# A hybrid decoder layer on one core: second-half norm by single tiles, two projections by turns, and a new order of small instructions on ScalarE and VectorE

## The chip, the cores and the metric

The kernel runs on one core of one Trainium2 chip. The metric is device time in microseconds (us) of one execution. The core has a matmul engine (TensorE, "PE" in the profile, its weight loads "PEld"), VectorE ("DVE"), ScalarE ("ACT"), GpSimd ("POOL") and SyncE ("SP", which issues DMAs). Each runs its own instructions strictly in the order in which they stand, and waits at semaphores for the others. Matmul results land in PSUM banks; a bank can be written again once DVE or ACT has copied it out.

## The reference, cut to what matters

One layer over 512 prompt rows and 8 x 4 sample rows, 1024 wide:

```python
x = layer_norm(ALPHA * x + 0.5 * swiglu(x, ffn1...), ln1_g, ln1_b)
proj = x @ w_in
ps_mix = ps + mu_shift * (prev - ps)           # prev: the row before
r, k, v, wd, ad, gd = slices of ps_mix
decay = exp(-exp(-softplus(-(w0 + tanh(wd) @ w_lora_up)) - 0.5))
a = sigmoid(a0 + ad @ a_lora_up);  g = sigmoid(gd) @ g_lora_up
kk = k * k_k;  kk = kk / max(sqrt(sum(kk * kk)), 1e-12)
k = k * (1 + (a - 1) * k_a)
o, wkv_new = wkv7_recurrence(r, decay, k, v, kk, a, wkv0)
y_rwkv = (group_norm(o) + sum(r * k * r_k) * v) * g
z = cw[0]*u[t-2] + cw[1]*u[t-1] + cw[2]*u[t];  y_conv = c_b * z      # u = c_c * c_h
x = layer_norm(ALPHA * x + concat(y_rwkv, y_conv) @ w_out, ln2_g, ln2_b)
x = layer_norm(ALPHA * x + 0.5 * swiglu(x, ffn2...), ln3_g, ln3_b)
```

## The kernel before

**Layout.** Channels lie on the 128 partitions, rows along the free axis: 544 rows in two halves, 256 (first) and 288 (second). Every weight matmul is done in three parts with both operands split into a rounded high half and a remainder: for each 128-channel tile of the input, `mm3` (L150 to L152) issues high x high, high x low, low x high. One projection of one half is 24 such matmuls. The split of an input tile is one ACT copy (L138) and one DVE subtraction (L139); the split of a weight tile is the pair L134, L135.

**The first norm.** `layer_norm` is run half by half. For the second half, once the reciprocal deviation is there (`rs`, two ACT instructions L255 and L258, tile `cpb`), it goes over the eight channel tiles in four pairs: DVE multiplies a pair (L262), ACT scales one tile (L268) and DVE the other (L266), then the pair is split for the projections. While that goes on, first-half projections fill PE; the second-half projections follow: 12 (`T12`, the inputs of decay and `a`), 13 (`sgd`, of the gate), 4 (`k` of pair 0), 0 (`r`).

**Projections.** `project` has 24 matmuls, then ACT evicts the bank (L880, L882, L883, tiles `pb` and `dt`), and DVE mixes each row with the one before (L884, L888).

**Pairs.** The eight heads are four pairs. For a pair, `gates` (L947, L950) makes the decay's sigmoid `sw` and `a`; `square` (L956) squares the pair's `k`; `norms` (L962, L963) sums the squares on PE and clamps them on DVE; `decays` makes a running sum on DVE (L969, tile `Pn`) and its exponentials on ACT (L974 to L978), with a table load ahead (L123); `prep` (L990 to L1001) makes the operands of the recurrence on DVE: `AR` and `nk` (the normalized keys), `a` rescaled (L994), the key times `a` (L997) and the products in `bkb` (L998, L999). ACT's sigmoids of the next pair write the tile of `a` that L997 is the last to read.

**Scores and chains.** `scores` (L1018 to L1061) makes each pair's triangular products, transposes `bkb` and `v` into `BK` and `UV`, and copies them out on ACT (L1037, L1053). `elim` solves small triangles on DVE and sends them over DRAM to `DM` and `O` (DMAs of L1093), from which `rounds` (L1123) doubles the block size on PE. Then a chain over eight chunks carries the state; in each chunk PE multiplies (L1195), DVE and ACT copy the result to `UV` (L1196, L1197), and PE goes on (L1204).

**Conv.** `conv` does the short convolution, three projections for each 128 channels; `conv_taps` holds the three taps: the first on ACT (L1335), the other two on DVE (L1337), each for the prompt's 512 columns and the samples' 32.

**What sets the order.** Each engine's instructions stand in the order in which the code issues them. `weave` and `drain` take background generators from a queue (`bg`) and put portions of their matmuls between the steps of a critical one; `seq` runs generators one after the other, `alt` lets them take turns at each of their `yield`s. A `tc.issue_after(x)` lets the instructions within it go behind `x` and not ahead; otherwise a scheduler is free to place an instruction anywhere its data allow. A pair's preparation runs as background (`own_a`, `own_b`) behind the pair before.

Of the kernel before, what the change touches and what calls it, by code (L numbers as in the profile page):

```python
# [19 lines left out]
P = 128  # L20
# [41 lines left out]
def body(ctx: ExitStack, tc: tile.TileContext, xT, gu1, wd1, win, wo_c, wo_0, wo_1, gu2, wd2, wl, ln3, eye, lora, vec, cst,  # L62
# [58 lines left out]
    def issue(prev, f, *args, **kw):  # L121
        with tc.issue_after(prev.ins):
            return f(*args, **kw)  # L123
# [32 lines left out]
    bg = deque()  # L156
    seen = dict(pe=None, fill=None, new=[], old=[])

# [53 lines left out]

    def layer_norm(z, c0, c1, gcol, bcol, epsv, q, rs, s1, sink, table=None, hl2=None, both=False):
        n = c1 - c0
# [44 lines left out]
        yield 1200 if pair else 600  # L259
        for d in range(0, KD, 2):  # L260
            zz = z[:, d:d + 2, c0:c1]
            DVE.tensor_tensor(zz, zz, rs[:, None, :n].to_broadcast([P, 2, n]), op=OP.mult)  # L262
            for e in (d, d + 1):
                x, g, b = z[:, e, c0:c1], col(gcol, e), col(bcol, e)
                if both and e > d:
                    DVE.tensor_scalar(x, x, g, b, op0=OP.mult, op1=OP.add)  # L266
# [22 lines left out]
    def to_x(spill):  # L289
        def sink(d, x, c0, c1):  # L290
            split(xhl[:, 0, d:d + 2, c0:c1], xhl[:, 1, d:d + 2, c0:c1], x)
            if spill:
                dma(xsp[:, d:d + 2, c0:c1], x)
        return sink
# [533 lines left out]
    drain()  # L828
    ln1b = layer_norm(z, *HALF[1], V_LN1G, V_LN1B, epsf, lnq, f1.lnr, f1.s1[1], to_x(True), None, f1.hl2, True)
    ss = keep.tile([P, 14, NSEQ], F32, name="sst")  # L830
# [32 lines left out]
    def s4(x):  # L863
        return x.rearrange("p (b t) -> p b t", t=4)

    def project(i, mt, h, x):
        c0, c1 = HALF[h]
        w = wget(i)
        q = big()
        yield from mm3(q[:, :c1 - c0], w, xhl, range(KD), c0, c1)  # L870
        pb = pp.tile([P, 297], F32, name="pb", bufs=2)
        d = pp.tile([P, 288], F32, name="dt", bufs=2)
        t0 = 256 * h
        pv = pb[:, 257:297].rearrange("p (b t) -> p b t", t=5)
# [5 lines left out]
        ACT.activation(pb[:, 1:257], q[:, :256], AF.Copy)  # L880
# [3 lines left out]
        DVE.scalar_tensor_tensor(x[:, t0:t0 + 256], pb[:, 0:256], col(V_MU, mt), d[:, 0:256], op0=OP.mult, op1=OP.add)  # L884
        if h == 0:
            POOL.tensor_copy(car[:, mt:mt + 1], pb[:, 256:257])
        else:
            DVE.scalar_tensor_tensor(s4(x[:, 512:544]), pv[:, :, 0:4], col(V_MU, mt), s4(d[:, 256:288]),  # L888
                                     op0=OP.mult, op1=OP.add)
# [44 lines left out]
    class Pair:  # L934
# [18 lines left out]

        def square(self, kf):
            self.kq = kq = p2.tile([P, 576], F32, name="kq")
            ACT.activation(kq, kf, AF.Square, scale=col(V_KK, self.p))  # L956

# [7 lines left out]
        def decays(self):  # L965
            p, kq = self.p, self.kq
            self.Pi = Pi = p2.tile([P, 600], F32, name="Pi")
            self.Pn = Pn = p2.tile([P, 576], F32, name="Pn")
            DVE.tensor_tensor_scan(Pn, keepm, self.sw, 0.0, op0=OP.mult, op1=OP.add)  # L969
# [4 lines left out]
            ln_exp(self.sg, lambda: ACT.activation(pi[:, :, 1:65], s64(Pn[:, :512]), AF.Exp, scale=-CDEC))  # L974
            ACT.activation(ps_[:, :, 1:5], s4(Pn[:, 512:]), AF.Exp, scale=-CDEC)
# [7 lines left out]
        def prep(self, kf, rf, vf):  # L983
# [12 lines left out]
            DVE.tensor_tensor(s4(AR[:, pl, 8, 1, :]), s4(rf[:, 512:]), ps_[:, :, 1:5], op=OP.mult)  # L996
            DVE.tensor_tensor(kf, kf, a, op=OP.mult)  # L997
            DVE.tensor_tensor(bkb[:, :, 1, :], s64(kf), s64(Pn), op=OP.mult)  # L998
            DVE.tensor_tensor(bkb[:, :, 0:3:2, :], s64(nk)[:, :, None, :].to_broadcast([P, NC_, 2, 64]),  # L999
                              s64(Pn)[:, :, None, :].to_broadcast([P, NC_, 2, 64]), op=OP.mult)  # L1000
            DVE.scalar_tensor_tensor(nk, rf, col(V_RK, p), kf, op0=OP.mult, op1=OP.mult)  # L1001

        def scores(self):
# [23 lines left out]
            for a0c, n in ((0, 5), (5, 4)):  # L1027
# [8 lines left out]
                for par, q in enumerate(qs):  # L1036
                    ACT.activation(BK[:, pl, par, a0c:a0c + m, :], s64(q[:, :64 * m]), AF.Copy)  # L1037
                    if a0c:
                        ACT.activation(BS[R(par), pl, 64 * par:64 * par + 64], q[R(par), 192:256], AF.Copy)
# [112 lines left out]
    def chain(g, cp, small):  # L1152
# [25 lines left out]
        for c in range(8):  # L1178
# [15 lines left out]
            for pl, par in heads:  # L1194
                crit(PE.matmul(at(qs[par], pl, par), XT[R(par), c, pl, :], W[R(par), pl, :], start=True, stop=True))  # L1195
            DVE.tensor_copy(UV[R(0), :, 0, c, :], v2(qs[0], R(0)))  # L1196
            seen["new"] = [ACT.copy(UV[R(1), :, 1, c, :], v2(qs[1], R(1)))]  # L1197
# [131 lines left out]
    def conv_taps(i, u, us, zc):  # L1329
        zs = s4(zc[:, TP:])  # L1330
        for t in range(3):
            wt = col(V_CW, 4 * t + i)
            for dst, src in ((zc[:, :TP], u[:, t:t + TP]), (zs, us[:, :, t:t + 4])):
                if t == 0:
                    ACT.activation(dst, src, AF.Copy, scale=wt)  # L1335
                else:
                    DVE.scalar_tensor_tensor(dst, src, wt, dst, op0=OP.mult, op1=OP.add)  # L1337
# [126 lines left out]
    def conv_last(i=3):  # L1464
# [13 lines left out]
        conv_taps(i, u, us, zc)  # L1478
        dma(conv_o, cvo)
# [170 lines left out]
```

## Time and profile before

| | us |
|---|---|
| median of 3 runs (lowest, highest) | 1086.52 (1081.96, 1087.96) |
| the profiled execution's own time | 1086.63 |
| its span in the trace | 1084.9 |
| PE busy | 1056.1 (97%) |
| DVE busy | 841.5 (78%) |
| ACT busy | 580.8 (54%) |
| POOL busy | 177.1 (16%) |

The rows of the timeline give the start, the time from start to end of the group (x says how many instructions are taken together), the engine, line, operation, the tiles written and read, their shape, and in brackets the idle time just before and what ended it. The rows of the windows give for a stretch of time the busy time of each engine with its instructions, then the clock that was granted to TensorE (1.00 is full speed), then the DMA engines' share and rate. Matmuls overlap, so the distance of two starts, not a matmul's own length, is what one costs.

### The profile page before, as it was taken

Reading aid. Unit: us, or ns where it says so; the run is one execution under the profiler, and the core shown is the slowest. Engines: PE = TensorE matmul, PEld = TensorE weight load, DVE = VectorE, ACT = ScalarE, POOL = GpSimd, SP = SyncE. Lnnn points to the kernel's source line nnn. Section 1 sums busy time; section 2 is a strip of 40 time slices with the busy share of each in tenths; the row PEclk is TensorE's granted clock in tenths of the full one; section 3 lists DMA queues with packets and bytes.
Section 4 is the critical chain, followed back from the end, with each engine's and each line's share of the span. In section 5 each row is a group of like instructions: output and inputs, shape, how many; then the busy total and the mean of one; then the engine's idle time right before and its main releaser. Section 6 shows DMA issues by size and latency. Waiting matters only on the chain.

```text
span 1084.9 us, 22650 instructions
## 1 busy us (share of the span) xinstructions
PE 1056.1 (97%) x9178; PEld 1014.3 (93%) x9178; DVE 841.5 (78%) x1548; ACT 580.8 (54%) x1074; POOL 177.1 (16%) x288
## 2 busy tenths in 40 slices
PE   9999999999999999999999999999999999999997
PEld 8999999999999997898879987899999999999996
DVE  6788888889775866785478657999988888888746
ACT  5745465555552667664444434667465555555523
POOL 0122220312200022132001200001212212121000
PEclk9999999999999999999999999999999999999999
DMA  8568595867854233234155724454775949678512
GB/s 295 123 126 191 118 220 130 176 157 147 189 120 151 82 107 83 65 85 85 50 148 158 183 65 128 163 155 79 146 187 122 224 105 198 150 152 188 152 45 83
DMA packets 96153, 150.00 MB, mean 138 GB/s; under 512 B 35120, under 2 KB 56752, under 8 KB 95920
## 3 DMA queue, kind: packets, MB, share of 16 engines
q1 hardware_dynamic: 68416, 111.81, 33.4%
q0 software_dynamic: 27200, 36.18, 21.9%
q8 instruction: 72, 1.18, 0.5%
q10 hardware_dynamic: 432, 0.56, 0.2%
q14 instruction: 33, 0.27, 0.1%
HBM read 129.86 MB, written 9.75 MB: 129 GB/s over the span
## 4 chain that ended last, share of the span: by engine, by line
PE 62%; issue 11%; DVE 9%; DMA 8%; ACT 8%; POOL 0%; ACTq 0%; POOLq 0%; DVEq 0%
PE mm L533 7%; PE mm L535 6%; PE mm L534 6%; PE mm L150 6%; PE mm L151 6%; PE mm L152 6%; DMA raw<-in_gu 5%; PE sm L535 4%; PE sm L534 4%; PE sm L533 4%; ACT hl L134 3%; DVE hl L135 2%; PE sm L1123 1%; DMA raw<-in_wd 1%; PE mm L754 1%
## 5 line engine op out<-in xcount | busy, mean ns | idle before, releaser
L135 DVE TENSOR_TENSOR hl<-raw,hl 128x1024 fp32r<-128x1024 f32 (+3 forms) x232 | 271.5, 1177 | 69.3 <-ACT hl L134 68.2
L134 ACT ACTIVATE hl<-raw 128x1024 fp32r<-128x1024 f32 (+3 forms) x232 | 232.8, 1018 | 87.0 <-DVE raw L500 40.8
L150 PE MATMUL mm<-xhl,hl 128*128 128x288 f32 (+1 forms) x704 | 211.1, 301 | 4.1 <-DVE z L1514 1.6
L151 PE MATMUL mm<-xhl,hl 128*128 128x288 f32 (+1 forms) x704 | 205.3, 292 | 0.3 <-DVE xhl L139 0.3
L152 PE MATMUL mm<-xhl,hl 128*128 128x288 f32 (+1 forms) x704 | 203.6, 290 | 0.1
L150 PEld LDWEIGHTS mm<-xhl,hl 128*128 128x128 f32 x704 | 133.4, 190 | 11.4 <-DVE z L1514 2.6
L151 PEld LDWEIGHTS mm<-xhl,hl 128*128 128x128 f32 x704 | 133.9, 190 | 2.7 <-issue 1.4
L152 PEld LDWEIGHTS mm<-xhl,hl 128*128 128x128 f32 x704 | 133.7, 190 | 1.2 <-issue 0.7
L535 PE MATMUL sm<-xhl,hl 128*128 128x272 f32 x432 | 125.5, 290 | 0.0
L534 PE MATMUL sm<-xhl,hl 128*128 128x272 f32 x432 | 124.6, 288 | 0.0
L533 PE MATMUL sm<-xhl,hl 128*128 128x272 f32 x432 | 124.2, 288 | 0.0
L533 PE MATMUL mm<-tv,hl 128*128 128x272 f32 x288 | 83.4, 290 | 3.8 <-ACT cpb L594 2.5
L506 POOL DMA_DIRECT2D raw<-in_gu x36 | 43.4, 1206 | 247.6 <-DVE hlb L139 161.0
L535 PE MATMUL mm<-tv,hl 128*128 128x272 f32 x288 | 83.5, 290 | 0.0
L534 PE MATMUL mm<-tv,hl 128*128 128x272 f32 x288 | 83.2, 289 | 0.0
L533 PEld LDWEIGHTS sm<-xhl,hl 128*128 128x128 f32 x432 | 81.5, 189 | 0.0
L534 PEld LDWEIGHTS sm<-xhl,hl 128*128 128x128 f32 x432 | 81.4, 188 | 0.0
L535 PEld LDWEIGHTS sm<-xhl,hl 128*128 128x128 f32 x432 | 81.4, 188 | 0.0
L512 POOL DMA_DIRECT2D raw<-in_wd x32 | 39.3, 1483 | 257.7 <-DVE hlb L139 231.1
L533 PEld LDWEIGHTS mm<-tv,hl 128*128 128x128 f32 x288 | 54.4, 189 | 5.3 <-ACT cpb L594 4.0
L533 PE MATMUL mm<-hhl,hl 128*128 128x272 f32 x192 | 57.0, 302 | 0.7 <-DVE z L623 0.7
L533 PE MATMUL sm<-hhl,hl 128*128 128x272 f32 x192 | 56.0, 292 | 0.0
(406 smaller groups left out, 2729.7 us busy)
## 6 DMA issues: line engine op xcount, KB each, us to landing
raw<-in_gu SPq DMA_DIRECT2D x84, 512.0 KB, 4.7
raw<-in_gu POOLq DMA_DIRECT2D x36, 512.0 KB, 6.7
raw<-in_wd SPq DMA_DIRECT2D x32, 512.0 KB, 5.2
raw<-in_win SPq DMA_DIRECT2D x26, 512.0 KB, 3.8
raw<-in_wd POOLq DMA_DIRECT2D x32, 256.0 KB, 7.2
z<-cpb POOLq DMA_DIRECT2D x16, 272.0 KB, 9.6
z<-sv POOLq DMA_DIRECT2D x16, 272.0 KB, 5.7
raw<-in_wo SPq DMA_DIRECT2D x8, 512.0 KB, 4.0
```

Source lines behind the costliest of these rows:

```text
L134: ACT.activation(hl[:, 0, a:b], raw[:, a:b], AF.Copy)
L135: return DVE.tensor_tensor(hl[:, 1, a:b], raw[:, a:b], hl[:, 0, a:b].bitcast(F32), op=OP.subtract)
L150: PE.matmul(out, wh, src[:, 0, k, c0:c1], start=(start and i == 0), stop=False)
L151: PE.matmul(out, wh, src[:, 1, k, c0:c1], start=False, stop=False)
L152: seen["fill"] = PE.matmul(out, wl, src[:, 0, k, c0:c1], start=False, stop=(stop and i == n - 1))
L506: POOL.dma_start(x.rearrange("p (s c) -> p s c", s=2), bass.AP(tensor=a11.tensor, offset=a11.offset, ap=[[2 * D, P], [P * 2 * D, 2], [1, 5 ...
L512: POOL.dma_start(four(x)[:, i], bass.AP(tensor=a11.tensor, offset=a11.offset, ap=[[DFF, P], [P * DFF, 2], [1, 256]]), accum_op=OP.add)
L533: PE.matmul(out, wh, src(0, i), start=(first and i == 0), stop=False, skip_group_check=True)
L534: PE.matmul(out, wh, src(1, i), start=False, stop=False, skip_group_check=True)
L535: PE.matmul(out, wl, src(0, i), start=False, stop=(i == n - 1), skip_group_check=True)
L754: seen["fill"] = PE.matmul(q[:, :n], x[:, y, m, tok], self.wm[m][:, v, c:c + n], start=False, stop=(m == n6 - 1 and i == 2), skip_group_ch ...
L1123: crit(PE.matmul(q[r0:r0 + m, o:o + nn], lhs, rhs, start=True, stop=True))
```

## The change

Six things are changed; what is computed stays the same.

1. In the second half of the first norm (`fine=True`) tiles 0 and 1 are done singly: DVE multiplies and scales each, then each is split alone. The other three pairs stay as they were. For these two tiles ACT has no scaling left (one L268 fewer), and DVE one L266 more.
2. Second-half projections 12 and 13 take turns (`alt`), so both use a data tile when it is there.
3. In `prep` the key times `a` is issued first and the two `bkb` products and the `nk` product behind it.
4. In `decays` the running sum stands behind the mixing of the pair's `k`, and the table load and so the exponentials stand behind the square.
5. For pair 2, the first two `BK` copies of `scores` go from ACT to DVE.
6. The two DVE taps of each conv are issued at two places of the third projection, each behind the last `UV` copy, instead of all at once.

```diff
-    def ln_exp(prev, first):
-        p = issue(prev, ACT.preload_act_table_set, "natural_log_exp_and_others")
+    def ln_exp(prev, first, also=None):
+        with tc.issue_after((also or prev).ins):
+            p = issue(prev, ACT.preload_act_table_set, "natural_log_exp_and_others")
...
-        for d in range(0, KD, 2):
+        for d in range(2 if fine else 0):
+            x = z[:, d, c0:c1]
+            DVE.tensor_tensor(x, x, rs[:, :n], op=OP.mult)
+            DVE.tensor_scalar(x, x, col(gcol, d), col(bcol, d), op0=OP.mult, op1=OP.add)
+            sink(d, z[:, d:d + 1, c0:c1], c0, c1)
+            yield 850
+        for d in range(2 if fine else 0, KD, 2):
...
-            split(xhl[:, 0, d:d + 2, c0:c1], xhl[:, 1, d:d + 2, c0:c1], x)
+            w = x.shape[1]
+            split(xhl[:, 0, d:d + w, c0:c1], xhl[:, 1, d:d + w, c0:c1], x)
...
-    drain(project(0, 12, 1, T12), project(1, 13, 1, sgd), project(2, 4, 1, kf), project(3, 0, 1, rf))
+    drain(alt(project(0, 12, 1, T12), project(1, 13, 1, sgd)), project(2, 4, 1, kf), project(3, 0, 1, rf))
...
         def square(self, kf):
+            self.mix = seen["mix"]
             self.kq = kq = p2.tile([P, 576], F32, name="kq")
-            ACT.activation(kq, kf, AF.Square, scale=col(V_KK, self.p))
+            self.sq = ACT.activation(kq, kf, AF.Square, scale=col(V_KK, self.p))
...
-            DVE.tensor_tensor_scan(Pn, keepm, self.sw, 0.0, op0=OP.mult, op1=OP.add)
+            with tc.issue_after(self.mix.ins):
+                DVE.tensor_tensor_scan(Pn, keepm, self.sw, 0.0, op0=OP.mult, op1=OP.add)
...
-            ln_exp(self.sg, lambda: ACT.activation(pi[:, :, 1:65], s64(Pn[:, :512]), AF.Exp, scale=-CDEC))
+            ln_exp(self.sg, lambda: ACT.activation(pi[:, :, 1:65], s64(Pn[:, :512]), AF.Exp, scale=-CDEC),
+                   self.sq)
...
-            DVE.tensor_tensor(kf, kf, a, op=OP.mult)
-            DVE.tensor_tensor(bkb[:, :, 1, :], s64(kf), s64(Pn), op=OP.mult)
...
+            ke = DVE.tensor_tensor(kf, kf, a, op=OP.mult)
+            with tc.issue_after(ke.ins):
+                DVE.tensor_tensor(bkb[:, :, 1, :], s64(kf), s64(Pn), op=OP.mult)
...
-                    ACT.activation(BK[:, pl, par, a0c:a0c + m, :], s64(q[:, :64 * m]), AF.Copy)
+                    src, dst = s64(q[:, :64 * m]), BK[:, pl, par, a0c:a0c + m, :]
+                    if p == 2 and not a0c:
+                        DVE.tensor_copy(dst, src)
+                    else:
+                        ACT.activation(dst, src, AF.Copy)
...
-        conv_taps(i, u, us, zc)
+        taps = conv_taps(i, u, us, zc)
+        next(taps)
         for h in range(2):
-            yield from conv_mm(16 + 3 * i, h, partial(conv_z, zc))
+            for n, x in enumerate(conv_mm(16 + 3 * i, h, partial(conv_z, zc))):
+                if n in (0, 2):
+                    next(taps, None)
+                yield x
+            for _ in taps:
+                pass
```

The line numbers below are those of each kernel, so the same instruction has a number that is higher by 1 to 26 in the changed one (L884, for one, is L892 there). The tile `z` is the norm's data, `cpb` its reciprocal deviation, `xhl` the split input of the projections, `v` and `T` projections' results.

DVE at the second half of the first norm, before:

```order
L262 TENSOR_TENSOR z<-z,cpb 128x2x288 x2
L266 TENSOR_SCALAR z<-z,vc 128x288 x2
L262 TENSOR_TENSOR z<-z,cpb 128x2x288
L139 TENSOR_TENSOR xhl<-z,xhl 128x2x288 x2
L884 SCALAR_TENSOR_TENSOR v<-pb,vc,dt 128x256
L266 TENSOR_SCALAR z<-z,vc 128x288
L262 TENSOR_TENSOR z<-z,cpb 128x2x288
```

and DVE at the same place in the changed kernel:

```order
L263 TENSOR_TENSOR z<-z,cpb 128x288 x2
L264 TENSOR_SCALAR z<-z,vc 128x288 x2
L269 TENSOR_TENSOR z<-z,cpb 128x2x288
L140 TENSOR_TENSOR xhl<-z,xhl 128x288 x2
L273 TENSOR_SCALAR z<-z,vc 128x288
L892 SCALAR_TENSOR_TENSOR v<-pb,vc,dt 128x256
L269 TENSOR_TENSOR z<-z,cpb 128x2x288
```

Two products of one tile each and their two scalings now stand first; the product of the second pair stands between these and the splits of tiles 0 and 1.

DVE at the end of pair 0's `prep` and the start of pair 1's norms, before (`k` and `Pn` are pair 1's from the running sum on):

```order
L994 TENSOR_SCALAR a<-a,vc,der 128x576
L999 TENSOR_TENSOR bkb<-nk,Pn 128x9x2x64
L997 TENSOR_TENSOR k<-k,a 128x576
L998 TENSOR_TENSOR bkb<-k,Pn 128x9x64
L1001 SCALAR_TENSOR_TENSOR nk<-r,vc,k 128x576
L969 SCALAR_TENSOR_TENSOR Pn<-keepm,sw 128x576
L884 SCALAR_TENSOR_TENSOR k<-pb,vc,dt 128x256 x2
L888 SCALAR_TENSOR_TENSOR k<-pb,vc,dt 128x32
```

and in the changed kernel:

```order
L1005 TENSOR_SCALAR a<-a,vc,der 128x576
L1008 TENSOR_TENSOR k<-k,a 128x576
L1011 TENSOR_TENSOR bkb<-nk,Pn 128x9x2x64
L1010 TENSOR_TENSOR bkb<-k,Pn 128x9x64
L1013 SCALAR_TENSOR_TENSOR nk<-r,vc,k 128x576
L892 SCALAR_TENSOR_TENSOR k<-pb,vc,dt 128x256 x2
L896 SCALAR_TENSOR_TENSOR k<-pb,vc,dt 128x32
L979 SCALAR_TENSOR_TENSOR Pn<-keepm,sw 128x576
```

The key times `a` moved ahead of one product, and the running sum (printed as SCALAR_TENSOR_TENSOR with `keepm`) behind the three mixings.

ACT at the same place, before (from pair 1's sigmoid of `a` to the exponentials; `kq` is the square of L956):

```order
L950 ACTIVATE a<-sm,vc 128x256
L950 ACTIVATE a<-sm,vc 128x320
L123 ACT_TABLE_LOAD
L880 ACTIVATE pb<-mm 128x256
L882 ACTIVATE pb<-mm 128x8x4
L883 ACTIVATE dt<-mm,omu 128x288
L974 ACTIVATE Pi<-Pn 128x8x64
L975 ACTIVATE Pi<-Pn 128x16x4
L134 ACTIVATE hl<-raw 128x1024
L956 ACTIVATE kq<-k,vc 128x576
L880 ACTIVATE pb<-mm 128x256
L883 ACTIVATE dt<-mm,omu 128x256
```

and in the changed kernel:

```order
L958 ACTIVATE a<-sm,vc 128x256
L958 ACTIVATE a<-sm,vc 128x320
L888 ACTIVATE pb<-mm 128x256
L890 ACTIVATE pb<-mm 128x8x4
L891 ACTIVATE dt<-mm,omu 128x288
L135 ACTIVATE hl<-raw 128x1024
L965 ACTIVATE kq<-k,vc 128x576
L123 ACT_TABLE_LOAD
L888 ACTIVATE pb<-mm 128x256
L891 ACTIVATE dt<-mm,omu 128x256
L984 ACTIVATE Pi<-Pn 128x8x64
L986 ACTIVATE Pi<-Pn 128x16x4
```

The table load and the two exponentials of `Pi` moved from ahead of the square to behind it. On PE the same stretch has pair 1's two `norms` matmuls 13 matmuls of `mm3` earlier than before: 13 that stood ahead of them stand behind them now.

More of the change, by code (lines that the diff above doesn't have):

```diff
@@ L156, in body @@
     bg = deque()
-    seen = dict(pe=None, fill=None, new=[], old=[])
+    seen = dict(pe=None, fill=None, uv=None, new=[], old=[])
     def crit(e):
@@ L211, in seq, with layer_norm @@
             yield from g
-    def layer_norm(z, c0, c1, gcol, bcol, epsv, q, rs, s1, sink, table=None, hl2=None, both=False):
+    def layer_norm(z, c0, c1, gcol, bcol, epsv, q, rs, s1, sink, table=None, hl2=None, both=False, fine=False):
         n = c1 - c0
@@ L887, in project @@
         else:
-            DVE.scalar_tensor_tensor(s4(x[:, 512:544]), pv[:, :, 0:4], col(V_MU, mt), s4(d[:, 256:288]),
-                                     op0=OP.mult, op1=OP.add)
+            seen["mix"] = DVE.scalar_tensor_tensor(s4(x[:, 512:544]), pv[:, :, 0:4], col(V_MU, mt), s4(d[:, 256:288]),
+                                                   op0=OP.mult, op1=OP.add)
             POOL.tensor_copy(sho[:, mt, 0:1], pb[:, 256:257])
@@ L1195, in chain @@
                 crit(PE.matmul(at(qs[par], pl, par), XT[R(par), c, pl, :], W[R(par), pl, :], start=True, stop=True))
-            DVE.tensor_copy(UV[R(0), :, 0, c, :], v2(qs[0], R(0)))
+            seen["uv"] = DVE.tensor_copy(UV[R(0), :, 0, c, :], v2(qs[0], R(0)))
             seen["new"] = [ACT.copy(UV[R(1), :, 1, c, :], v2(qs[1], R(1)))]
@@ L1332, in conv_taps @@
             wt = col(V_CW, 4 * t + i)
[L1333 to L1337, printed above, removed]
+            with ExitStack() as st:
+                if t and seen["uv"] is not None:
+                    st.enter_context(tc.issue_after(seen["uv"].ins))
+                for dst, src in ((zc[:, :TP], u[:, t:t + TP]), (zs, us[:, :, t:t + 4])):
+                    if t == 0:
+                        ACT.activation(dst, src, AF.Copy, scale=wt)
+                    else:
+                        DVE.scalar_tensor_tensor(dst, src, wt, dst, op0=OP.mult, op1=OP.add)
+            yield 0
         POOL.tensor_copy(cvo[:, i, 0:2], u[:, TP:TP + 2])
@@ L1477, in conv_last @@
             yield from conv_mm(15 + 3 * i, h, partial(conv_u, cc, u, us))
-        conv_taps(i, u, us, zc)
+        for _ in conv_taps(i, u, us, zc):
+            pass
         dma(conv_o, cvo)
```

10 lines of the change are left out of this document (5 added, 5 removed).

## The prediction

> **What bounds the kernel now.** First the busy times of the page, with the span:
>
> ```profile
> span 1084.9 us, 22650 instructions
> PE 1056.1 (97%) x9178; PEld 1014.3 (93%) x9178; DVE 841.5 (78%) x1548; ACT 580.8 (54%) x1074; POOL 177.1 (16%) x288
> ```
>
> The change takes no matmul away, so PE's stream can shorten only where PE idles (28.8 us in all) or runs at a lower clock. Next, PE's waits (engine, line, what released it: total, times, longest):
>
> ```profile
> PE sm L1204 <- DVE UV L1196: 3.7, 8, 1.0
> PE sm L962 <- ACT kq L956: 1.9, 1, 1.9
> PE mm L150 <- ACT xhl L138: 1.5, 1, 1.5
> PE sm L1032 <- ACT BK L1037: 1.0, 1, 1.0
> ```
>
> These are the places that the change touches: the norm's second half (L150), pair 1's norms (L962), pair 2's scores (L1032), and one chunk of the chain (L1204). Then the windows around them, for PE busy and granted clock (0.50 or 1.00, ahead of DMA share and rate):
>
> ```profile
> 288.06:291.48 3.42, 2.37 (x19) 2.16 (x19) 2.55 (x6) 2.00 (x3) 0.00 (x0) 1.00 0.59 100
> 291.48:294.89 3.41, 3.41 (x29) 3.41 (x29) 3.38 (x5) 3.04 (x5) 0.00 (x0) 1.00 0.72 221
> 390.46:393.88 3.42, 1.67 (x11) 1.22 (x11) 3.42 (x7) 3.12 (x7) 0.39 (x1) 1.00 0.36 124
> 393.88:397.29 3.41, 3.41 (x16) 3.41 (x15) 3.09 (x7) 2.35 (x4) 1.26 (x3) 0.50 0.73 155
> 424.60:428.01 3.41, 1.50 (x12) 1.27 (x10) 2.48 (x5) 3.40 (x9) 1.18 (x6) 1.00 0.01 2
> 428.01:431.42 3.41, 3.39 (x9) 2.58 (x9) 1.97 (x4) 1.65 (x4) 0.59 (x3) 0.50 0.39 132
> 564.54:567.96 3.42, 2.39 (x33) 1.71 (x32) 1.79 (x2) 2.83 (x8) 0.00 (x0) 1.00 0.37 81
> 567.96:571.37 3.41, 3.41 (x11) 2.84 (x12) 1.13 (x3) 1.96 (x8) 0.00 (x0) 0.50 0.51 154
> ```
>
> Behind three of these waits the clock is 0.50 for 3.41 us, in which PE does half the work: 1.7 us lost each time, as much as the wait itself. PE idled 1.75, 1.91 and 1.03 us in the windows ahead. In the last, PE's 33 instructions are mostly of 64 columns and rows; among long matmuls 1.05 us of idle (window at 288.06) left the clock at 1.00. So the idle from which the half clock follows lies, for long matmuls, between 1.05 and 1.75 us. The first two waits are at chains of ACT and DVE, the third at ACT behind a DMA.
>
> **The first norm's second half.** The rows, PE's first and then DVE's, with a window of PE at full work on 288 columns:
>
> ```profile
> 392.64 0.53 PE L150 MATMUL mm<-xhl,hl 128*128 128x288 f32 x2 [1.50 <-ACT xhl L138]
> 389.92 1.43 DVE L262 TENSOR_TENSOR z<-z,cpb 128x576 f32<-128x576 f32 x2 [0.31 <-ACT cpb L258]
> 391.27 0.77 DVE L266 TENSOR_SCALAR z<-z,vc 128x288 f32<-128x288 f32 x2
> 404.12:407.53 3.41, 3.41 (x27) 3.32 (x26) 0.00 (x0) 3.38 (x6) 0.51 (x4) 1.00 0.77 251
> ```
>
> Before, PE starts when the first pair's high half is done (392.64), having idled since 391.14. After: two single products from 389.92, at some .39 (half a pair's product is .36, one scaling on DVE .39), then two scalings of .39: tile 0 is ready at about 391.1. ACT's copy of one tile costs some .45, estimated from its sigmoids of 256 columns (.89 for two, below), so PE gets high halves at 391.6, 1.0 earlier. The remainders come later: the second pair's product (.72) stands ahead of their splits, so the first is there at 392.5. Until then PE has the matmuls of both projections on high halves, at .13 each (26 to 27 in 3.41 at full clock); I put its idle time at 0.5 to 1.2 and take 0.95. That is under the 1.05, so I take the half-clock stretch at 393.88 as gone: it held 16 matmuls, 10 fewer, so 1.3. Together PE is (1.75 - 0.95) + 1.3 = 2.1 ahead. ACT has one scaling less, DVE three operations more; ACT then idles 3.40 before the next eviction (next rows), which covers them.
>
> What PE gains here must pass the gates:
>
> ```profile
> 400.23 0.39 ACT L880 ACTIVATE pb<-mm 128x256 f32<-128x256 f32 x1 [3.40 <-PE mm L152]
> 408.32 0.78 ACT L956 ACTIVATE kq<-k,vc 128x576 f32<-128x576 f32 x1 [0.79 <-DVE k L888]
> 411.43 1.28 ACT L123 ACT_TABLE_LOAD   x1
> 413.38 0.69 DVE L995 TENSOR_TENSOR AR<-r,Pi 128x512 f32<-128x512 f32 x1 [1.00 <-ACT Pi L974]
> 414.60 0.80 PE L947 MATMUL sm<-T,cpb 64*128 64x320 f32 x2 [0.24 <-DVE kq L963]
> ```
>
> From the first eviction (400.23) to the table load (411.43) ACT works nearly without a break: 11.2 us, in which it idles 0.79 once, a wait that goes when PE is ahead; 10.4 remain. Two projections taking turns end together, so the first eviction comes only 0.8 earlier though PE is over 2 ahead. The table load so comes 0.8 + 0.8 = 1.6 earlier, 1.8 with the small gaps between instructions. DVE's clamp (L963) stands behind L995, which waits for `Pi`, and frees the bank that PE's last gate matmuls need: they move from 414.60 by 1.8 at most, and PE, 2.1 ahead, waits about 0.5 there where it waited 0.24. Gain up to here: 1.8; between 0.8 (evictions no earlier than PE's idle time allows) and 2.1 (all).
>
> **Pair 1's preparation.** The chain to its norms:
>
> ```profile
> 420.59 1.35 DVE L999 TENSOR_TENSOR bkb<-nk,Pn 128x1152 f32<-128x1152 f32 x1
> 421.86 0.75 DVE L997 TENSOR_TENSOR k<-k,a 128x576 f32<-128x576 f32 x1
> 424.05 1.35 DVE L969 TENSOR_TENSOR_SCAN Pn<-keepm,sw 128x576 f32<-128x576 f32 x1
> 425.31 0.98 DVE L884 SCALAR_TENSOR_TENSOR k<-pb,vc,dt 128x256 f32<-128x256 f32 x2
> 422.64 0.89 ACT L950 ACTIVATE a<-sm,vc 128x256 f32<-128x256 f32 x2 [2.25 <-DVE k L997]
> 427.20 0.78 ACT L956 ACTIVATE kq<-k,vc 128x576 f32<-128x576 f32 x1
> 428.03 2.29 PE L962 MATMUL sm<-kq,cs 128*128 128x256 f32 x4 [1.93 <-ACT kq L956]
> 431.45 0.38 PE L1018 MATMUL sm<-AR,bkb 64*128 64x128 f32 x2
> ```
>
> ACT's sigmoid waits for L997, which stands behind the 1.35 of L999; moved ahead, it frees `a` 1.35 earlier. The table load, two exponentials and a weight split, all between that sigmoid and the square before, lie behind the square now except for the split (1.06), which fits while DVE mixes. DVE's mixing, before at 425.31 behind the running sum (1.35), now comes without it, and needs ACT's eviction of `k`, which also is 1.35 earlier and freed of the table load. Its last row ended at 426.3, a short one of the samples' columns behind it; so the mixing ends 1.8 + 1.35 earlier, at 423.3, and the square (.78) at 424.1, where before it was done at 427.98: the norms start 3.9 earlier. But 13 matmuls stand behind them that stood ahead: 13 x .13 = 1.7. PE, 1.8 ahead and without these 13, comes to the norms at 426.1 - 3.5 = 422.6 and waits some 1.5 (before 1.93). That is between 1.05 and 1.75; since this window also has long matmuls on both sides of the wait, I take the full clock behind it, the least certain step. What was done from 428.03 to 431.45 at half clock takes half, 1.7; with the 13, the first score matmul starts at 424.1 + 1.7 + 1.7 = 427.5. Gain from the start to here 3.9, with the 1.8 in it.
>
> The running sum and the exponentials come later now; they feed `prep` of pair 1, which has the whole of pair 0's scores as cover. For pair 2 the running sum (1.35) and a weight split (1.23) stand ahead of the last steps of pair 0's elimination, which so ends up to 2.6 later. Its way over DRAM, and the first matmul that reads `O`:
>
> ```profile
> L1093 SPq DMA_DIRECT2D O<-Dd x4: 1165/1734/2717, 487.0 to 608.6; - x4
> DMA to landing us min/median/max: 5.0/6.0/8.0
> L1123 PE MATMUL sm<-O,DM x128: 217/219/254, 501.6 to 622.4; 64*64 64x48 f32 x128
> ```
>
> The first of two is issued at 487.0, the second at most 2.7 behind; with 8.0 it lands by 497.7, so 3.9 are left to 501.6. Cost nothing; were the cover gone, up to 2.6.
>
> **Chain and scores.**
>
> ```profile
> 547.49 1.74 DVE L1337 SCALAR_TENSOR_TENSOR zc<-cu,vc,zc 128x512 f32<-128x512 f32 x4
> 549.14 0.28 DVE L1196 COPY UV<-sm 64x128 f32<-64x128 f32 x1
> 565.08 1.06 ACT L134 ACTIVATE hl<-raw 128x1024 fp32r<-128x1024 f32 x1 [4.88 <-DMA raw<-in_win]
> 566.04 0.74 ACT L1037 ACTIVATE BK<-sm 128x320 f32<-128x320 f32 x2
> 566.81 0.89 ACT L1053 ACTIVATE UV<-sm 64x320 f32<-64x320 f32 x2
> 566.16 1.23 DVE L135 TENSOR_TENSOR hl<-raw,hl 128x1024 fp32r<-128x1024 f32 x1 [1.92 <-ACT hl L134]
> ```
>
> The four taps hold the `UV` copy until 549.14. The second pair of taps (half of 1.74) now stands behind it, so it may start .87 earlier, if its matmuls are done by then; of PE's wait of 1.0 there I take 0.7 as gone, 0.87 at most. The weight split pushed behind the taps feeds a later projection; nothing is gained or lost by it.
>
> At pair 2's scores ACT is held by a weight split that waits for its DMA until 565.08; the `BK` copies stand behind it and PE behind them. DVE idles 1.92 there, so two copies of about .37 cost it nothing and are done by 565.0 (its idle time begins at 564.24). Next to be late is the `UV` copy on ACT, still behind that split, which starts at 566.04 instead of 566.81. Gain 0.8, between 0 (the split comes later) and 1.03; with a wait of about 0.3 the half clock at 567.96 goes too: 1.7.
>
> **The sum.** 3.9 + 0.7 + 0.8 + 1.7 = 7.1, from 1086.6 of the profiled execution: **1079.5**. That execution and the median of the runs (1086.52) agree within 0.1.
>
> [...]
>
> **Rivals.**
>
> *A stretch comes back.* PE still waits some 0.95 at the norm, 1.5 at pair 1's norms and 0.3 at the scores, and the grid of 3.41 us may or may not cut a wait in two. One returned stretch of 1.3 to 1.7 gives 1081.1, two 1082.7. For it: 1.5 is over 1.05. Against it: 1.5 is under 1.75, and no other is over 1.05. Chance .30.
>
> *The half clock is not from these waits.* Then the stretches stay where they are, being due to something that the change does not touch. PE's 0.8 at the norm is swallowed by ACT's chain, the 13 matmuls eat the rest at the norms, and 0.7 + 0.8 = 1.5 are left: 1085.1. Against it: in each of the three it follows directly behind a wait. Chance .12. [...]
>
> *The square comes no earlier.* If ACT's eviction of `k` is late (a PSUM bank, a weight split that waits for its DMA), the norms' 13 matmuls are moved behind a wait that has stayed: 1.7 lost, the half clock stays there, and 0.7 + 0.8 + 1.7 are gained elsewhere: 1085.1. It decides when the square is done later than 428.0 - 1.7 = 426.3; I have 424.1. Chance .08.
>
> *Slower: the grid hits elsewhere.* The three stretches start 34.13 (10 x 3.413) and 139.95 (41 x 3.413) apart, so on a fixed grid; a program that is several us ahead behind 431 is cut by it at other places. At the eight chunks PE waits 3.7 in all for `UV`, with short matmuls between, as in the window at 564.54. If five of these windows now fall to the half clock that did not before, 5 x 1.7 = 8.5 are lost and the time is 1088.0; from more than four on it is slower than before. For it: the runs of before lie 6 us apart, 3.5 stretches; against it: before, none of these was at half clock in the trace. Chance .06.
>
> **How the numbers follow.** The forecast has .44. Faster or slower by 0.5% (5.4 us; about what a measurement can tell here) means below 1081.1 or above 1091.9. The forecast lies 1.6 inside the first bound, and I count .40 of its .44; of the returned stretches one alone is on the bound, .10. Slower takes the grid rival's tail and what I have not seen, .07. The range goes from 1076.8 (2.1 up to the gates, 0.87 at the `UV` copy, and the waits of 0.95, 1.5 and 0.3 that I left standing shorter by 2.2 in all) to 1086.2 (the rivals at 1085.1 with an error of 1); outside are the grid rival and what lies beyond.
>
> **What the changed profile would show.** Right: PE's first second-half matmul at about 391.6; clock 1.00 at 393.88, 424 to 431 and 568; the gates' last matmuls starting at 412.8, behind a wait for the clamp; pair 1's square at 423.3, its norms at 424.1 and the first score matmul at 427.5; the `UV` copy ahead of the second taps; `BK` done by DVE while ACT waits. Wrong: a window at 0.50 at any of these, or a score matmul later than 429; or the gain there by 430 and lost again by 500, at a wait of the rounds for `O` or `DM`.

## The result, and the profile after

The changed kernel takes 1086.74 us (median of 21 runs, 1084.11 to 1091.42), the kernel before 1085.42 in as many runs: ratio 1.001, 95% interval 0.9996 to 1.0024. No gain, where 1079.5 was forecast and 1086.2 was the upper end. The profiled execution took 1089.17 (before 1086.63).

The page's first lines, and of PE's waits those that bear on the change (engine, line, what released it: total, times, longest):

```profile
span 1087.4 us, 22652 instructions
PE 1055.6 (97%) x9178; PEld 1013.9 (93%) x9178; DVE 842.0 (77%) x1553; ACT 579.9 (53%) x1072; POOL 179.2 (16%) x288
```

```profile
PE sm L971 <- ACT kq L965: 4.7, 2, 3.2
PE sm L1220 <- DVE UV L1212: 3.0, 8, 0.6
PE sm L1139 <- issue: 2.1, 1, 2.1
PE sm L955 <- DVE kq L972: 1.1, 1, 1.1
PE sm L1064 <- ACT UV L1069: 0.7, 1, 0.7
PE mm L151 <- ACT xhl L139: 0.5, 1, 0.5
```

The waits that the change aimed at have shrunk (the norm's 1.5 to 0.5, `UV` 3.7 to 3.0, `BK`'s 1.0 to 0.7 at `UV`). Two have grown or are new. The norms (L971, before L962) now wait twice, 1.5 at pair 1 and 3.2 somewhere else; and PE waits 2.1 in the rounds (L1139) for nothing that the profile names. The gates' wait for the clamp (L955) is 1.1, where about 0.5 was forecast.

The timeline shows that the first part went as forecast, to 0.4 us (this execution began 0.2 ahead of that of before, which is not yet taken off here):

```profile
391.46 0.53 PE L151 MATMUL mm<-xhl,hl 128*128 128x288 f32 x2 [0.49 <-ACT xhl L139]
392.36 0.40 PE L152 MATMUL mm<-xhl,hl 128*128 128x288 f32 x1 [0.37 <-DVE xhl L140]
412.90 0.80 PE L955 MATMUL sm<-T,cpb 64*128 64x320 f32 x2 [1.07 <-DVE kq L972]
423.36 0.78 ACT L965 ACTIVATE kq<-k,vc 128x576 f32<-128x576 f32 x1 [1.32 <-DVE k L896]
424.19 1.24 PE L971 MATMUL sm<-kq,cs 128*128 128x256 f32 x4 [1.50 <-ACT kq L965]
427.74 2.16 PE L1030 MATMUL sm<-AR,bkb 64*128 64x128 f32 x33
```

Forecast were 391.6, 412.8, 423.3, 424.1 and 427.5. The first score matmul (L1030) is 3.7 ahead of the kernel before (3.5 without the early start), and so is all of PE up to 483. Then the second wait of the norms, at pair 3. Its chain, back from PE over ACT, DVE and GpSimd:

```profile
492.16 1.24 PE L971 MATMUL sm<-kq,cs 128*128 128x256 f32 x4 [3.17 <-ACT kq L965]
491.33 0.77 ACT L965 ACTIVATE kq<-k,vc 128x576 f32<-128x576 f32 x1 [3.25 <-DVE k L896]
490.61 0.53 DVE L892 SCALAR_TENSOR_TENSOR k<-pb,vc,dt 128x256 f32<-128x256 f32 x1 [6.17 <-POOL pb L884]
490.38 0.19 POOL L886 COPY pb<-car 128x1 f32<-128x1 f32 x1
490.14 0.18 POOL L894 COPY car<-pb 128x1 f32<-128x1 f32 x1
487.13 1.93 POOL L1198 COPY S<-UV 64x128 f32<-64x128 f32 x6 [11.34 <-DMA Dd<-AT]
```

Each row waits for the next one. DVE can mix the second half of pair 3's `k` only when GpSimd has put the carried row into `pb` (L886, 0.19 us). (The bracket of DVE names L884, a small write just behind L886 that ends within 0.1 us of it; in the code it is L886 that writes what this mixing reads.) L886 stands behind ten copies for the chain (`S` and `SI`), and the first of these waits 11.34 for the DMA that reads `AT`, the elimination's result. (`S` needs nothing of `AT`; it lies in the memory that `AT` gives up, as the order of the pools in the code has it.) The same places in the kernel before:

```profile
492.53 1.21 PE L962 MATMUL sm<-kq,cs 128*128 128x256 f32 x4
491.67 0.79 ACT L956 ACTIVATE kq<-k,vc 128x576 f32<-128x576 f32 x1
490.94 0.48 DVE L884 SCALAR_TENSOR_TENSOR k<-pb,vc,dt 128x256 f32<-128x256 f32 x1 [2.69 <-POOL pb L876]
487.03 2.02 POOL L1182 COPY S<-UV 64x128 f32<-64x128 f32 x6 [7.63 <-DMA Dd<-AT]
```

There the first copy began at the same time, 487.03, and DVE waited for GpSimd too, 2.69. But PE came to the norms 3.5 later, and the square (done at 491.67 + 0.79 = 492.46) was ready less than 0.1 ahead of it. So PE had no wait, and nothing to spare either.

SyncE's queue says why the DMA came no earlier (start, time to issue). First before, then after:

```profile
482.07 0.38 SPq L1089 DMA_DIRECT2D Dd<-De  x1
482.50 1.25 SPq L1090 DMA_DIRECT2D Dd<-AT  x1
483.84 1.71 SPq L117 DMA_DIRECT2D raw<-in_win  x1
485.65 1.32 SPq L1093 DMA_DIRECT2D DM<-Dd  x2
```

```profile
479.96 0.33 SPq L117 DMA_DIRECT2D raw<-in_win  x1
480.59 0.38 SPq L1105 DMA_DIRECT2D Dd<-De  x1
481.02 2.77 SPq L1106 DMA_DIRECT2D Dd<-AT  x1
485.71 1.32 SPq L1109 DMA_DIRECT2D DM<-Dd  x2
```

The elimination ends only 1.5 earlier, while PE is 3.7 earlier, and a weight load of 512 KB now stands ahead of its DMAs instead of behind. The DMA of `AT` lands 4.4 after its start before, and 6.0 after it now: at 486.9 and at 487.0. DVE's rows of the changed kernel show what stands directly ahead of the elimination's first step (L1100):

```profile
458.66 1.35 DVE L979 TENSOR_TENSOR_SCAN Pn<-keepm,sw 128x576 f32<-128x576 f32 x1
459.93 1.20 DVE L136 TENSOR_TENSOR hl<-raw,hl 128x1024 fp32r<-128x1024 f32 x1
461.05 0.17 DVE L1100 TENSOR_TENSOR tm<-AT,De 128x15 f32<-128x15 f32 x1
```

The first is pair 2's running sum, which the kernel before has much earlier, at 450.06 (the weight split stood here before, too). Between the elimination's first and last step there is besides one weight split (1.22) more than before, and one product of the conv (0.41).

### The profile page after: what moved, and what is told of

It reads as the page before. It is cut to its first block, busy times and chain, and to the rows that moved or that the text cites. A ratio compares the mean times of both kernels' runs of the same rounds, so it can differ in the third digit from the quotient of the medians.

```text
span 1087.4 us, 22652 instructions
## 1 busy us (share of the span) xinstructions
PE 1055.6 (97%) x9178; PEld 1013.9 (93%) x9178; DVE 842.0 (77%) x1553; ACT 579.9 (53%) x1072; POOL 179.2 (16%) x288
## 3 DMA queue, kind: packets, MB, share of 16 engines
q8 instruction: 72, 1.18, 0.4%
## 4 chain that ended last, share of the span: by engine, by line
PE 66%; DVE 10%; issue 9%; DMA 7%; ACT 7%; POOL 1%; ACTq 0%; POOLq 0%; DVEq 0%
PE mm L541 8%; PE mm L542 7%; PE mm L543 7%; PE mm L151 6%; PE sm L543 5%; PE sm L542 5%; PE sm L541 5%; PE mm L152 5%; PE mm L153 5%; DMA raw<-in_gu 3%; ACT hl L135 2%; DVE hl L136 2%; PE sm L1139 1%; DMA raw<-in_wd 1%; PE mm L762 1%
```

## The experiments

To compare executions, this table has the start of the same matmuls in each, in us ahead (-) of the profiled execution of before; the lead that an execution has at 387.7, where the code is still the same in all, is taken off. The columns: end of pair 1's gates, then the first matmuls of pair 3's gates (482), of the rounds (498), of pair 2's and of pair 3's scores (560, 579), of the second rounds (617), and of the second chain's samples (638). Half-clock windows are those between 390 and 660.

| execution | 415 | 482 | 498 | 560 | 579 | 617 | 638 | half clock from |
|---|---|---|---|---|---|---|---|---|
| before | 0 | 0 | 0 | 0 | 0 | 0 | 0 | 393.9, 428.0, 568.0 |
| e7 (before) | 0.0 | -1.6 | -1.6 | -1.6 | -3.3 | -3.3 | -2.4 | 394.1 |
| e8 (before) | 0.0 | 0.0 | 0.0 | 0.0 | -0.1 | -0.1 | -0.1 | 395.7, 429.8, 569.8 |
| e6 (before, GpSimd's copies behind) | 0.0 | 0.0 | 0.0 | +0.5 | +0.4 | +0.4 | +0.3 | 394.1, 428.2, 568.2 |
| changed | -1.5 | -3.5 | -0.2 | -0.9 | -3.0 | -3.0 | +2.4 | 623.9 (10.2 us) |
| e4 (changed) | -1.6 | -3.5 | -0.5 | -1.2 | -1.9 | -1.9 | -1.5 | 564.8 |
| e1 | -1.6 | -3.6 | -3.6 | -4.3 | -6.7 | -6.6 | -4.8 | 636.1 |
| e2 | -1.5 | -3.6 | +1.2 | +2.7 | +1.0 | +1.1 | +0.9 | 492.7, 523.4 |
| e3 | -1.5 | -1.5 | -1.5 | -2.3 | -4.5 | -4.5 | -4.4 | 425.8 |
| e5 | -1.5 | -3.6 | -3.6 | -3.0 | -3.2 | -3.1 | -2.8 | 413.4, 563.5 |
| e9 | -1.5 | -3.6 | -3.6 | -4.2 | -6.6 | -6.5 | -5.2 | none |
| e10 | -1.5 | -1.6 | -1.6 | -2.3 | -4.6 | -4.5 | -4.0 | 423.7 |
| e11 | -1.5 | -3.3 | -3.3 | -2.5 | -4.9 | -4.9 | -5.3 | 519.1 |
| e12 | -1.6 | -3.3 | -3.3 | -4.0 | -6.5 | -6.5 | -0.8 | 619.3 (10.2 us) |

**e1: GpSimd's copies behind.** The changed kernel, with the copies for the first chain (`S`, and `SI` in the same way) put behind pair 3's last `sho` copies.

```diff
-                    POOL.tensor_copy(Sn[R(1 - par), :, par, :], UV[R(1 - par), :, par, c + 1, :])
+                    after(POOL.tensor_copy(Sn[R(1 - par), :, par, :], UV[R(1 - par), :, par, c + 1, :]), seen["sho"])
...
+            seen["sho"] = POOL.tensor_copy(sho[:, mt, 1:9], pv[:, :, 4])
```

> The changed kernel with ten GpSimd copies (the first chain's S and SI) put behind pair 3's last sho copies instead of ahead of pair 3's car and pb copies; nothing else moves. Theory POOL: in the changed kernel the 3.7 us gained by 483 is lost at pair 3's norms because GpSimd's S copy waits for the DMA that reads AT (until 487.1) and the small pb copies stand behind it. Then PE's wait of 3.17 at pair 3's norms falls under 0.5, the first matmul of the rounds starts at about 494 (497.30 in the changed kernel), and the time is about 3 lower than the changed kernel's: 1083.5, ratio to before 0.998. Rival DMA: the same DMA holds the rounds too (DM, O land late), so the wait only moves there: the rounds start no earlier than 497, time unchanged. Rival clock: the loss is in half-clock stretches, not here: unchanged within 1.

1080.77, ratio to before 0.997 (0.9955 to 0.9986). The norms' waits in its list of waits:

```profile
PE sm L971 <- ACT kq L965: 1.5, 1, 1.5
```

Only pair 1's wait is left; the rounds start at 493.94 (494 expected). The 3.2 was this queue: PE, DVE, ACT and SyncE have the same instructions in the same order as in the changed kernel, and only GpSimd's order differs.

**e2 and e5: norm and pair part alone, without and with e1's move.** e2 is the changed kernel with `BK` on ACT and the taps all at once:

```diff
-                    if p == 2 and not a0c:
-                        DVE.tensor_copy(dst, src)
-                    else:
-                        ACT.activation(dst, src, AF.Copy)
+                    ACT.activation(dst, src, AF.Copy)
...
-        taps = conv_taps(i, u, us, zc)
-        next(taps)
+        for _ in conv_taps(i, u, us, zc):
+            pass
```

> The changed kernel without the BK copies on VectorE and without the dealt taps: only norm, alternating projections, prep order, running sum and table load. Theory POOL: PE is 3.7 ahead at 483 and 0.3 ahead from 492 on, and stays so to the end apart from the clock: ratio to before 0.999 to 1.001 (1085 to 1087). Rival clock: the three stretches at half clock that go bring 3 to 5 us whatever stands at pair 3: ratio 0.996.

e5 is e2 with e1's two edits.

> The kernel of e2 (norm, alternating projections, prep order, running sum, table load; no BK copies on VectorE, no dealt taps) with the ten GpSimd copies put behind pair 3's last sho copies as in e1. Theory POOL: the 3.7 to 4.0 that e2 had at 483 stays: the first matmul of the rounds is 3.7 ahead of the kernel before, and the time is about 3 below e2's (1.0008), so ratio 0.9975 to 0.9985 (1082). Rival clock: of the 3.7, 3.0 are half clock that the one profiled execution of before happened to have at 393.88 and 428.01; against the median of before only 1 is left, ratio 0.999 to 1.000.

e2: 1085.9, 1.0008 (0.9986 to 1.003); the lead of 3.6 is gone at the rounds, as expected, and half clock behind the wait (492.7) takes more. e5: 1081.55, 0.9978 (0.9956 to 1.0); the lead stays.

**e3: `BK` and taps alone.** The kernel before with only e2's lines the other way round.

> The kernel before with only the BK copies of pair 2 on VectorE and the dealt taps. Theory: 0.7 at the UV copy and 2.1 at pair 2's scores, as the changed kernel showed between 534 and 579 (from 0.3 ahead to 3.2 ahead), kept if the second rounds do not take it back: 2.8, ratio 0.9975 (1083). Rival: the second rounds (PE's wait put down to issue, and the half clock behind it) take it back because they start earlier: ratio 1.000 or over.

1081.13, 0.9985 (0.9968 to 1.0001): less sure a gain than expected. The steps are there, 0.7 ahead at the `UV` copy and 2.2 at pair 2's scores. But its lead at 415 is 1.5, with the code of before: that is the half clock at 394, which did not come.

**e4, e7, e8: the same kernels again.** No edit.

> The changed kernel once more, for a second profile. Theory chance: PE's wait of 2.05 in the second rounds at 621.5 and the half clock from 623.9 to 634.1 belong to that one execution; here the wait is 0.2 to 0.3 as before and the profiled execution takes about 1084. Rival fixed: they belong to the changed kernel, which starts its second rounds 3.15 earlier; the wait is 2 again and the profiled execution takes about 1089.

> The kernel before once more, for a second profile. Theory grid: the half clock falls by chance on the waits; the waits of 1.5, 1.9 and 1.0 are there again to 0.1, but at least one of the stretches at 393.88, 428.01 and 567.96 is gone or one is elsewhere, and the time moves by 1.7 for each from 1086.6. Rival: the waits bring the half clock each time: the same three stretches, 1086 to 1087.

> The kernel before a third time, as e7: theory grid and rival as there.

e4: 1082.97, 0.9989 (0.9966 to 1.0012); the wait in the rounds is 0.6 and the long half clock absent, so these do not belong to the code (for the wait 0.2 to 0.3 had been expected). e8 has the three stretches and 1086.83; e7 has one of them and 1083.1. The windows of e7 tell how near the bound lies (sum of PE busy, and the clock after the five busy times):

```profile
390.71:394.12 3.41, 1.62 (x11) 1.19 (x10) 3.41 (x7) 3.03 (x7) 0.30 (x1) 1.00 0.33 114
394.12:397.53 3.41, 3.41 (x17) 3.41 (x16) 3.09 (x7) 2.44 (x5) 1.36 (x3) 0.50 0.59 179
424.84:428.25 3.41, 1.61 (x13) 1.38 (x11) 2.48 (x5) 3.40 (x9) 1.17 (x6) 1.00 0.01 2
428.25:431.66 3.41, 3.29 (x35) 2.92 (x37) 2.15 (x5) 2.54 (x6) 0.59 (x3) 1.00 0.39 120
```

The grid lies 0.1 earlier against the same wait of 1.9, PE is busy 1.61 instead of 1.50 in the window, and the half clock does not follow; at the norm it followed on 1.62. And in e3 the wait of 1.50 at the norm is cut by the grid:

```profile
388.20:391.62 3.42, 1.93 (x16) 1.72 (x15) 3.11 (x7) 2.55 (x5) 0.32 (x2) 1.00 0.08 27
391.62:395.03 3.41, 3.14 (x23) 2.88 (x22) 3.37 (x7) 2.81 (x7) 1.66 (x3) 1.00 0.59 205
395.03:398.44 3.41, 3.41 (x28) 3.41 (x27) 1.02 (x3) 1.48 (x5) 0.31 (x2) 1.00 0.96 267
```

**e6: GpSimd's copies behind, in the kernel before.** e1's edits alone.

> The kernel before with only the ten GpSimd copies put behind pair 3's last sho copies. Theory POOL: in the kernel before PE does not wait at pair 3's norms, so nothing is gained: ratio 0.999 to 1.001 (1084 to 1086). Rival: the copies hold something else too, and the gain of e1 comes with them alone: ratio 0.997.

1084.57, 0.9985 (0.9964 to 1.0005), and in its profile the same leads as before (0.0 at 482 and 498): nothing to gain where PE does not wait there. The interval holds the rival's 0.997 too, so it is the profile that speaks against the rival, and not the time.

**e9: loads ahead.** e1, with two weight loads of the output projection issued ahead of two `y` loads. The lines shown are the middle of the edit; by it some splits on DVE and ACT get another place too.

```diff
...
+            for key, src in ((("0", 1), wo_0[1]), (("c", 2), wo_c[2])):
+                pre[key] = raw_tile()
+                dma(pre[key], src)
             ys = [(k, yload(k)) for k in (0, 1)]
...
```

> The kernel of e1 with two weight loads of the output projection (wo, 512 KB each) issued ahead of the two y loads on SyncE's queue, where e1 has them behind; so they land before the second rounds instead of during them. Theory fetch: PE's wait in the second rounds, put down to issue (2.05 in the changed kernel, 2.08 in e1, 0.0 to 1.2 elsewhere), is for a packet of the instruction queue that stands behind these loads on the DMA engines; it is 0.3 or less now, and the median is 0.5 to 1.5 below e1's 1080.8. Rival: the wait has nothing to do with the loads: 0.5 or more remains, median as e1.

1080.51, 0.9971 (0.9953 to 0.9989). The wait put down to issue is gone, but a new wait of 1.2 beside it took most of the gain. It is not the `y` loads that are late (they land at 612.9 and 613.5, and at 612.8 and 613.5 in e1). It is DVE's split of the `y` tiles, which began at 613.93 in e1 and begins at 616.72 here, behind four instructions of the rounds (L1148, L1154) that stood behind it in e1.

```profile
617.50 0.39 PE L152 MATMUL mm<-xhl,hl 128*128 128x256 f32 x1 [1.24 <-DVE xhl L140]
618.57 1.45 PE L1139 MATMUL sm<-XT,DM 64*32 64x32 f32 x72
```

**e10, e11: e1 without the norm part, and without the pair part.** e10 takes `fine` and `alt` away (first diff); e11 takes the new order of `prep`, running sum and table load away (second):

```diff
-    ln1b = layer_norm(z, *HALF[1], V_LN1G, V_LN1B, epsf, lnq, f1.lnr, f1.s1[1], to_x(True), None, f1.hl2, True, True)
+    ln1b = layer_norm(z, *HALF[1], V_LN1G, V_LN1B, epsf, lnq, f1.lnr, f1.s1[1], to_x(True), None, f1.hl2, True)
...
-    drain(alt(project(0, 12, 1, T12), project(1, 13, 1, sgd)), project(2, 4, 1, kf), project(3, 0, 1, rf))
+    drain(project(0, 12, 1, T12), project(1, 13, 1, sgd), project(2, 4, 1, kf), project(3, 0, 1, rf))
```

```diff
-            ke = DVE.tensor_tensor(kf, kf, a, op=OP.mult)
-            with tc.issue_after(ke.ins):
-                DVE.tensor_tensor(bkb[:, :, 1, :], s64(kf), s64(Pn), op=OP.mult)
...
+            DVE.tensor_tensor(kf, kf, a, op=OP.mult)
+            DVE.tensor_tensor(bkb[:, :, 1, :], s64(kf), s64(Pn), op=OP.mult)
...
-            with tc.issue_after(self.mix.ins):
+            if True:
                 DVE.tensor_tensor_scan(Pn, keepm, self.sw, 0.0, op0=OP.mult, op1=OP.add)
...
-            ln_exp(self.sg, lambda: ACT.activation(pi[:, :, 1:65], s64(Pn[:, :512]), AF.Exp, scale=-CDEC),
-                   self.sq)
+            ln_exp(self.sg, lambda: ACT.activation(pi[:, :, 1:65], s64(Pn[:, :512]), AF.Exp, scale=-CDEC))
```

> The kernel of e1 without the single tiles in the norm and without the alternating projections. Theory: PE's wait of 1.5 in the norm and its half clock are back; prep order, running sum and table load alone make the square of pair 1 1.35 earlier, with 13 matmuls moved behind it, so the first score matmul is 1 to 2 ahead of the kernel before, most of it the half clock that goes at 428; the whole 2 above e1: ratio to before 0.9985.

> The kernel of e1 with the old prep order, running sum and table load. Theory: PE is 2.5 to 3 ahead at the gates of pair 1 as in e1, 1.7 at their end; the square of pair 1 is 1.8 ahead, so the first score matmul is 1.8 to 2 ahead of the kernel before (3.7 in e1): ratio 0.9985 to 0.999. Rival: PE's gain at the norm is swallowed by ScalarE, and the score matmul is under 1 ahead.

e10: 1080.0, 0.9979 (0.9959 to 0.9999). Its lead goes from 1.5 at 415 (half clock at 394 absent) to 1.6 at 482, with half clock behind the norms as before: the pair part alone brought 0.1. e11: 1078.45, 0.9949 (0.9929 to 0.9969), better than expected, though its interval overlaps e1's; 3.3 ahead at 482, and nearly all that e1 has there is the norm part with what goes of the half clock.

**e12: norm part, `BK` and taps.** The changed kernel without the pair part, GpSimd's copies in their old place.

> The changed kernel without its pair part (old prep order, running sum and table load) and with the GpSimd copies where they were: e11 without the GpSimd move. Theory pair part: it is the pair part that puts a weight load ahead of the elimination's DMAs on SyncE's queue and a running sum and a weight split ahead of the elimination's last steps on VectorE; without it the DMA that reads AT lands 3.5 earlier than in the kernel before (487.0), PE's wait at pair 3's norms is 0.3 or less, and the median is that of e11, 1078 to 1080.5, ratio 0.995 to 0.997. Rival: any kernel whose PE is 3 ahead at 483 runs into GpSimd's copies; the wait is 2 to 3 and the median 1082 to 1084.

1078.82, 0.995 (0.9923 to 0.9977): as fast as e11, with nothing in it but parts of the change. SyncE's queue and GpSimd's first copy in it:

```profile
476.95 0.38 SPq L1103 DMA_DIRECT2D Dd<-De  x1
477.38 0.89 SPq L1104 DMA_DIRECT2D Dd<-AT  x1
478.52 1.65 SPq L117 DMA_DIRECT2D raw<-in_win  x1
481.59 2.17 POOL L1196 COPY S<-UV 64x128 f32<-64x128 f32 x6 [7.32 <-DMA Dd<-AT]
```

The weight load is behind the elimination's DMAs again, and the copy begins 5.4 to 5.5 earlier than in the kernel before and the changed one, of which about 1.5 is this execution's own early start. So it is the pair part that makes the elimination late. In e12's trace pair 2's running sum is back at its early place, at 445.2, and the additional weight split among the elimination's steps is gone. Which of the pair part's three edits does it was not tried.

## Why the prediction was wrong

**Norm and gates: right.** PE idled 0.86 (0.95 forecast), the half clock behind it went (in none of the eight profiles with the norm part is there any at 390 to 400), and the gates' chain left 1.5 of 2.4 (1.8 of 2.1 forecast).

**Pair 1: right in its times, 3.5 against 3.9.** The square, the norms' wait of 1.50 and the full clock behind it came as forecast. The 13 matmuls moved behind the norms cost what the earlier square brought: without the clock, 0.1 (e10) to 0.3 (e1 against e11) is left.

**"Cost nothing": the step that failed.** The prediction saw that pair 2's running sum and a weight split stand ahead of the elimination's last steps, and priced it at nothing, since the rounds' first use of `O` left 3.9. It asked only PE, the reader of what the DMAs bring. GpSimd waits for one of these DMAs, to reuse the memory that it reads, and pair 3's small copies wait behind it. In the trace of before this stood in two rows, the `S` copy's wait of 7.63 for `Dd<-AT` and DVE's wait of 2.69 for GpSimd; that PE did not wait there then was because PE was late. 3.3 of 3.5 were taken back. The text named the place in its last lines (gain by 430, lost by 500), but at a wait of the rounds, and gave it no chance of its own and no place in the sum. Undoing this step alone (e1) brings the ratio from 1.001 to 0.997: a gain of some 3 of the 7.1 forecast. What is still missing is put down to the clock, below.

**Taps and `BK`: right.** 0.7 forecast, 0.7 at the last `UV` copy in each kernel that has them (the changed one, e1, e3, e4, e9, e10, e11, e12). At pair 2's scores 2.5 forecast, 2.2 to 2.5 found, and 0.8 in e4, which has half clock there; without half clock on either side 0.7 of it is `BK` (2.4 in e1 against 1.7 in e7).

**The clock: right in kind, wrong as a sum.** Of the 7.1, 1.3 + 1.7 + 1.7 = 4.7 were half clock that the profiled execution had. e7 has one of the three stretches and runs 3.5 faster on the same code; so the kernel before has them in some executions only, and a median holds the part that occurs. The table counts it. At the norm the old code has the stretch in 4 of 6 profiles, the new in 0 of 8; behind pair 1's norms it is 4 of 5 with both parts old and 0 of 6 with both new; at pair 2's scores 4 of 6 with `BK` on ACT and 1 of 8 with `BK` on DVE. So the change does remove them at these places, but only what was there on average could be gained: the medians of before, for the result and beside the experiments, are 1083.1 to 1085.4, not the 1086.6 that the sum started from. Against an execution of before without half clock (1.5 + 1.6 ahead at 482) the changed kernel's 3.5 is a gain of 0.4, and e1's 6.7 at 579 is one of 1.9; the 3 us or so that its ratio shows lie between these two.

The grid rival was right that such stretches come elsewhere: 564.8, 623.9, 492.7 in kernels that have the change. Nor do they only follow waits, as the prediction took it: in e1 the half clock from 636.05 follows a window in which PE is busy throughout, with many short matmuls (e2 at 523.4 and e11 at 519.1 likewise):

```profile
632.64:636.05 3.41, 3.41 (x102) 3.25 (x98) 2.19 (x5) 1.83 (x6) 0.79 (x2) 1.00 0.40 156
636.05:639.47 3.42, 3.42 (x18) 3.29 (x16) 1.35 (x5) 0.08 (x1) 0.00 (x0) 0.50 0.51 156
```

How much idle time brings half clock is not shown by these runs: a window of 3.41 us with PE busy for 1.50 to 1.67 was followed by it at most places, one with 1.61 was not at two (e7, and the changed kernel at 487.38), nor were those with 1.67 and 1.69 in e11 and e12. What sets it stays open.

**The profiled execution's other 5.4** (617 to 638: from 3.0 ahead to 2.4 behind) is a wait in the second rounds and three windows at half clock behind it:

```profile
620.50:623.91 3.41, 1.36 (x65) 1.22 (x64) 0.94 (x3) 0.36 (x1) 0.00 (x0) 1.00 0.04 12
623.91:627.33 3.42, 3.42 (x92) 3.01 (x87) 1.38 (x6) 0.63 (x3) 0.00 (x0) 0.50 0.02 5
627.33:630.74 3.41, 2.82 (x22) 2.22 (x22) 0.59 (x3) 0.67 (x3) 0.00 (x0) 0.50 0.49 154
630.74:634.15 3.41, 3.26 (x20) 3.14 (x21) 1.10 (x4) 0.12 (x1) 0.00 (x0) 0.50 0.02 5
```

e4 has the same code without it, and e12 has it again without the pair part; so it comes and goes, and is no cost of the pair part. The changed kernel and e4, the same code, have ratios of 1.001 and 0.9989; their intervals overlap, so the runs show no difference between them.

## What to carry to other kernels

Where a step is delayed that ends in a DMA, list all who wait for that DMA, also those that only want its memory back, and what is queued behind each of them; a wait that cost nothing because PE was late turned into a price here, 3.2 at pair 3's norms, as soon as PE was 3.5 early. Do not book half-clock stretches of one profile as a gain (of the three here, e7 had one): profile the same kernel two or three times, and count the part that recurs. And try the parts of a bundle apart: here one part of three took back what the others gave.

## What the runs showed of the hardware

PE seems to wait for a packet of instructions; that is an estimate from the times below, and no run shows it directly. The wait of the rounds stands in each execution that has it behind the same 50th of 72 matmuls:

```profile
620.51 1.00 PE L1139 MATMUL sm<-XT,DM 64*32 64x32 f32 x50
623.57 0.79 PE L1139 MATMUL sm<-XT,DM 64*32 64x32 f32 x22 [2.05 <-issue]
```

In the trace a packet of 16 KB on the instruction queue starts at 621.38 and takes 0.97; PE goes on 1.2 after its end. In e7 the packet ends at 621.66 and PE goes on at 622.89, in e1 at 618.57 and 620.00: 1.2 and 1.4 after. The later the packet, the longer the wait: it starts 7.2 after the rounds' first matmul in the changed kernel, 6.3 in e7 and 5.2 in before, where the wait is 0.25; in e12 it is 7.3 and the wait 2.35, in e11 4.8 and there is none. The page of the changed kernel counts 72 packets and 1.18 MB on this queue (q8, of the kind "instruction"); what this one packet holds is not shown. By execution the wait is 0 to 2.4.

What delays the packet is not shown. Two weight loads are under way there, and in e9, with these loads ahead, it starts 2.7 after the rounds and there is no wait. But this is one profile, e11 has no wait with the loads where they were, and the time that the second load takes to land does not go with the packet: 8.3 in the changed kernel, but 6.9 in both e11 and e12, the shortest wait and the longest.
